# A hybrid trunk layer in fp32 on one core: the output projection's rows split in place in a ring of two slots, and the attention values of two head pairs copied together

## The chip, the cores and the metric

The kernel runs on one core of a Trainium2 chip. Its engines are TensorE (PE, matmuls; PEld is its weight load), VectorE (DVE), ScalarE (ACT), GpSimd (POOL) and SyncE (SP), which issues nearly all DMAs. Each engine, and each queue of issues, executes in the order in which the program was built. The metric is the time of one execution in microseconds (us).

## The reference: what is computed

One layer for 1024 tokens with 1024 channels, all float32:

```python
h = rmsnorm(x, ln1)
u_pool, gq, gk, gv, gg, ga, fq, fk, fv, ff = split(h @ w_in)
mix = concat(pool_mixer(u_pool), gla_mixer(gq, gk, gv, gg, ga), fox_mixer(fq, fk, fv, ff))
x = x + mix @ w_o
gate, up = split(rmsnorm(x, ln2) @ w_gu)
x = x + (silu(gate) * up) @ w_down
return rmsnorm(x, ln_f)
```

The pool mixer (256 channels) takes trailing means over 2, 4, 8 and 16 tokens, the gated linear attention (GLA, 4 heads of 64) runs over chunks of 64 tokens with a decayed state, and the forgetting attention ("fox", 8 heads of 64) is a causal softmax with an added decay `F_t - F_s`. The inner width of the FFN is 2816.

## The kernel before

**Products.** An fp32 matrix enters PE as a high half (rounded to float32r by ACT) and a low half (the raw value minus the high half, by DVE or POOL). A product is three matmuls: high by high, high by low, low by high. So each weight tile costs a load, one ACT rounding (line 118) and one subtraction (line 119) before PE can use it.

**Memory.** The large tiles are all of 128 partitions by 1024 floats. `G(name)` takes one of 33 slots from a list in the order in which slots were freed, and `free` gives it back. `R(name, tag)` takes the next slot of a ring: "p" has 6, "pp" 3, "fb" 2, "wr" (raw weights) 2, "w" (split weights) 4. A tile in a slot waits until the last use of the one before it is done. PSUM has banks "s" 3, "pt" 2, "o" 1 and "gm" 2; projections (`z...`, `psv`, `pxa`, `pxb`) all use the two "gm" banks.

**The program.** (1) Norm of x, its transposes `hT`, and the projection of the GLA values and the gates, up to about 60 us. (2) Pool inputs (`zp0`, `zp1`) and the GLA for head pairs A (j = 0) and B (j = 1): for each pair `keys` (`zgk`), `queries` (`zgq`) and `gates` (`zgg`). Small pieces of work are woven in between the matmuls of a projection: `state` (PE pkv, then a chain of 15 DVE updates of `St` at line 397), `within` (PE pat, then masked copies into `attb` at line 418), `outputs`, `turned`, and the pool's products (`py`, `pa`, `mh`). (3) `fox_values(0)`: the attention values of pairs 0 and 1, eight token blocks of 256 columns each (PE `psv0_0` to `psv0_7`), with pieces of GLA pair B between them. (4) For each pair p of fox heads: `fox_qk(p)` (`zq`, `zk`: projections whose results are split into q, k, kl) and `fox_attend(p)` (scores, softmax, transposes `pt`, the splits `pp` and the products `o`). PE fills the waits of a pair's attention with the projections of the next: psv1, zq2 and zk2 during pair 1, zq3 and zk3 during pair 2. (5) The output projection: `pxa` (first four blocks of `w_o`, with the tiles `mix`) and `pxb`. (6) Norm, FFN (`m`, 541 to 954 us), down projection (`d`, 954 to 1130 us), final norm.

**What the change touches.** `keep_wo(k)` (lines 279 to 284) splits the rows 128k to 128k+127 of `w_o`: load `wos{k}r`, round into `wos{k}h`, subtract into `wos{k}l`, and store both to a DRAM buffer `wod`, from which `fetch_wo` (line 289) takes them back for `pxa` and `pxb`. Each call takes three G slots, and gives them back when its reads are done. The eight calls follow `fox_values(0)` in the program. `fox_values` (lines 517 to 530) writes V tiles of one pair each, two per pair with four token blocks in a tile: for each token block and each pair one ACT copy (line 528, 128 x 128) and one DVE subtraction (line 529). The V tiles of a pair are freed when that pair's attention is done.

**What sets the order.** The kernel's text gives the program, and the tile framework's scheduler (`schedule_with_timeline_sim=True`) orders the instructions of all engines by its own estimate of when they become ready. Rows of engines can therefore move though the text that writes them did not.

## Time and profile before

| what | before |
|---|---|
| median of 3 runs | 1175.11 us (1174.69 to 1177.39) |
| profiled execution | 1175.42 us |
| its span in the trace | 1173.7 us |
| mean granted PE clock | 0.992 |
| PE busy | 1136.0 us (97%) |
| DVE busy | 828.2 us (71%) |
| ACT busy | 536.0 us (46%) |
| POOL busy | 340.4 us (29%) |
| HBM read, written | 105.09 MB, 44.34 MB |

The span is the part of the execution that the trace covers; the profiled time is 1.7 us longer. Busy shares overlap, since the engines work side by side. A row of waits names the instructions that stood, and the one whose end released them. In a row of the chain the time of an instruction is its own contribution to the end. A matmul row's "zq0p L152" is an instruction of line 152 that writes the tile zq0p.

### The profile page before, as it was taken

Reading aid. Unit: us, or ns where it says so; the run is one execution under the profiler, and the core shown is the slowest. Engines: PE = TensorE matmul, PEld = TensorE weight load, DVE = VectorE, ACT = ScalarE, POOL = GpSimd, SP = SyncE. Lnnn points to the kernel's source line nnn. Section 1 sums busy time; section 2 is a strip of 40 time slices with the busy share of each in tenths; the row PEclk is TensorE's granted clock in tenths of the full one; section 3 lists DMA queues with packets and bytes.
Section 4 is the critical chain, followed back from the end, with each engine's and each line's share of the span. In section 5 each row is a group of like instructions: output and inputs, shape, how many; then the busy total and the mean of one; then the engine's idle time right before and its main releaser. Section 6 shows DMA issues by size and latency. Waiting matters only on the chain.

```text
span 1173.7 us, 15953 instructions
## 1 busy us (share of the span) xinstructions
PE 1136.0 (97%) x5928; PEld 958.5 (82%) x5928; DVE 828.2 (71%) x1365; ACT 536.0 (46%) x970; POOL 340.4 (29%) x260
## 2 busy tenths in 40 slices
PE   6999998999999999998999999999999999999996
PEld 5877878889978888886888888888888888888875
DVE  6697364387746866579997767767686685876686
ACT  6454233466654644456453433444344344334345
POOL 2231123343322413210302221022201370660784
PEclk9999999999999999999999999999999999999999
DMA  7121184411203734431323332242314688333233
GB/s 250 37 73 52 59 295 174 176 39 35 91 18 126 305 132 159 173 112 46 117 86 129 101 115 88 101 134 82 135 54 152 224 322 293 103 95 102 86 112 143
DMA packets 57692, 150.45 MB, mean 128 GB/s; under 512 B 5080, under 2 KB 5512, under 8 KB 57616
## 3 DMA queue, kind: packets, MB, share of 16 engines
q1 hardware_dynamic: 57184, 147.87, 36.5%
q0 software_dynamic: 432, 1.57, 0.4%
q8 instruction: 46, 0.75, 0.3%
q14 instruction: 30, 0.25, 0.1%
HBM read 105.09 MB, written 44.34 MB: 127 GB/s over the span
## 4 chain that ended last, share of the span: by engine, by line
PE 76%; DVE 4%; DMA 1%; issue 1%; POOL 1%; ACT 1%; SPq 0%; POOLq 0%; DVEq 0%; ACTq 0%
PE m L774 36%; PE d L1030 15%; PE pxa L144 4%; PE pxb L144 3%; PE o L615 3%; PE pt L601 2%; PE psv L152 2%; PE s L575 1%; PE s L576 1%; PE zq3p L152 1%; PE zq0p L152 1%; PE zq2p L152 1%; PE zk1p L152 1%; PE zk2p L152 1%; PE zk0p L152 1%
## 5 line engine op out<-in xcount | busy, mean ns | idle before, releaser
L774 PE MATMUL m<-hA_0h,wr 128*128 128x512 f32 x616 | 214.7, 391 | 1.2 <-ACT hr L729 1.2
L774 PE MATMUL m<-hA_1h,wr 128*128 128x512 f32 x616 | 214.9, 389 | 0.0
L774 PEld LDWEIGHTS m<-hA_0h,wr 128*128 128x128 f32 x616 | 116.1, 189 | 25.8 <-ACT hr L729 1.6
L774 PEld LDWEIGHTS m<-hA_1h,wr 128*128 128x128 f32 x616 | 115.8, 188 | 24.2
L1030 PE MATMUL d<-lw,ha 128*128 128x512 f32 x308 | 119.9, 389 | 0.9 <-DVE lw L880 0.9
L774 PE MATMUL m<-hA_0l,wr 128*128 128x512 f32 x308 | 120.3, 391 | 0.0
L774 PE MATMUL m<-hA_1l,wr 128*128 128x512 f32 x308 | 119.9, 389 | 0.0
L1030 PE MATMUL d<-hw,ha 128*128 128x512 f32 x308 | 119.3, 389 | 0.0
L1030 PE MATMUL d<-hw,la 128*128 128x512 f32 x308 | 118.4, 389 | 0.0
L756 ACT ACTIVATE wr<-ws 128x512 fp32r<-128x512 f32 x110 | 69.5, 632 | 101.5 <-DVE ws L755 50.1
L826 POOL TENSOR_TENSOR cg<-cu,cu 128x512 f32<-128x512 f32 x11 | 19.7, 1795 | 302.8 <-DVE cu L803 266.7
L757 DVE TENSOR_TENSOR wr<-ws,wr 128x512 fp32r<-128x512 f32 x110 | 76.8, 704 | 20.6 <-ACT wr L756 20.5
L880 DVE TENSOR_TENSOR la<-ra,ha 128x1024 fp32r<-128x1024 f32 (+1 forms) x42 | 57.2, 1368 | 32.0 <-ACT ha L879 24.7
L590 POOL TENSOR_TENSOR pb<-pb,rl 128x128 f32<-128x128 f32 (+3 forms) x32 | 39.0, 1222 | 117.5 <-DVE rl L587 108.9
L872 POOL TENSOR_TENSOR rw<-wd,wd 128x512 f32<-128x512 f32 x33 | 59.0, 1815 | 47.7 <-PE d L1030 47.6
L879 ACT ACTIVATE ha<-ra 128x1024 fp32r<-128x1024 f32 (+1 forms) x42 | 41.3, 987 | 65.6 <-DMA ra<-cd 56.8
L1030 PEld LDWEIGHTS d<-lw,ha 128*128 128x128 f32 x308 | 57.8, 188 | 13.3 <-DVE lw L880 1.3
L604 DVE TENSOR_TENSOR pp<-pt,pp 128x512 fp32r<-128x512 f32 (+1 forms) x80 | 50.2, 631 | 25.7 <-ACT pp L603 25.3
L774 PEld LDWEIGHTS m<-hA_0l,wr 128*128 128x128 f32 x308 | 58.1, 189 | 12.0
L774 PEld LDWEIGHTS m<-hA_1l,wr 128*128 128x128 f32 x308 | 58.0, 188 | 12.0
L1030 PEld LDWEIGHTS d<-hw,la 128*128 128x128 f32 x308 | 57.8, 188 | 12.1
L1030 PEld LDWEIGHTS d<-hw,ha 128*128 128x128 f32 x308 | 57.8, 188 | 11.9
(398 smaller groups left out, 2690.6 us busy)
## 6 DMA issues: line engine op xcount, KB each, us to landing
ra<-cd SPq DMA_DIRECT2D x35, 512.0 KB, 3.9
wu<-in_w_gu_dram SPq DMA_DIRECT2D x22, 512.0 KB, 4.6
wg<-in_w_gu_dram SPq DMA_DIRECT2D x22, 512.0 KB, 3.7
wd<-in_w_down_dram SPq DMA_DIRECT2D x22, 512.0 KB, 6.4
mix<-mixs SPq DMA_DIRECT2D x14, 512.0 KB, 5.3
cd<-cg SPq DMA_DIRECT2D x11, 512.0 KB, 6.3
cd<-cs SPq DMA_DIRECT2D x11, 512.0 KB, 3.4
cd<-cu SPq DMA_DIRECT2D x11, 512.0 KB, 3.3
```

The costliest lines, as they stand in the source:

```text
L144: PE.matmul(ps, a, b, start=(n == 0), stop=(n == last))
L152: PE.matmul(ps, a, b, start=(i == 0 and n == 0), stop=(i == len(terms) - 1 and n == 2))
L590: POOL.tensor_tensor(out=pb[:, 0:W], in0=pb[:, 0:W], in1=rl[:, 0:1].broadcast_to([P, W]), op=ALU.mult)
L604: DVE.tensor_tensor(out=pp[:, 512:512 + w], in0=pt[:, 0:w], in1=f(pp[:, 0:w]), op=ALU.subtract)
L615: PE.matmul(*args, start=(kb == 0 and n_ == 0), stop=(last and n_ == 1))
L756: ACT.activation(hi, src, AF.Copy)
L757: DVE.tensor_tensor(out=lo, in0=src, in1=f(hi), op=ALU.subtract)
L774: PE.matmul(ps, a, b, start=(n == 0), stop=(n == 11))
L872: POOL.tensor_tensor(out=raw_[:, j * 512:j * 512 + 512], in0=wd[h0, j0 + j][:, e0, :], in1=wd[h1, j0 + j][:, e1, :], op=op)
L879: ACT.activation(hi[:, sl], src, AF.Copy)
L880: DVE.tensor_tensor(out=lo[:, sl], in0=src, in1=f(hi[:, sl]), op=ALU.subtract)
L1030: PE.matmul(banks[t], a[:, o], b[:, ns], start=(j0 + j == 0 and m == 0), stop=(j0 + j == NF // 2 - 1 and m == 2))
```

## The change

`keep_wo` takes two slots of the ring "fb" and no G slot: the raw rows land in the first, the high half goes into the second, and the low half is written over the raw rows. Both are stored. The ring has only these two slots, so the load of block k+1 can start when the low half of block k is stored. The same ring holds the squares of the first norm (before) and the decay sums that each attention pair broadcasts (`fb{p}_{a}`, behind). The eight calls stand earlier: two before the keys of B, two before its gates, four before `fox_values(0)`.

`fox_values` makes four V tiles that hold both pairs, with two token blocks in a tile, and copies both pairs of a token block at once (128 x 256): one ACT and one DVE instruction in place of two and two. The four tiles are freed together when the odd pair is done; before, a pair's two tiles were freed after that pair. While pair 2 and pair 3 are worked on, pair 2's values therefore stay two slots longer.

```diff
     def keep_wo(k):
 
-        hi, lo = load_g(w_o[k * P:(k + 1) * P, :], f"wos{k}", tag="G")
+        raw, hi = R(f"wos{k}", tag="fb"), R(f"wosh{k}", F32R, tag="fb")
+        SP.dma_start(raw, w_o[k * P:(k + 1) * P, :])
+        ACT.activation(hi, raw, AF.Copy)
+        DVE.tensor_tensor(out=raw, in0=raw, in1=f(hi), op=ALU.subtract)
         SP.dma_start(wod[k, :, 0], f(hi))
-        SP.dma_start(wod[k, :, 1], f(lo))
-        free(f"wos{k}h", f"wos{k}l")
+        SP.dma_start(wod[k, :, 1], raw)
...
-        V = [[G(f"v{2 * q + j}_{i}", F32R).rearrange("p (t h s e) -> p t h s e", t=4, h=2, s=2) for i in range(2)] for j in range(2)]
+        V = [G(f"v{q}_{i}", F32R).rearrange("p (t j h s e) -> p t j h s e", t=2, j=2, h=2, s=2) for i in range(4)]
...
-            for j in range(2):
-                v_ = V[j][tb // 4][:, tb % 4]
-                pv = ps[:, 128 * j:128 * j + 128].rearrange("p (h e) -> p h e", h=2)
-                ACT.activation(v_[:, :, 0], pv, AF.Copy)
-                DVE.tensor_tensor(out=v_[:, :, 1], in0=pv, in1=f(v_[:, :, 0]), op=ALU.subtract)
+            v_ = V[tb // 2][:, tb % 2]
+            pv = ps[:, 0:256].rearrange("p (j h e) -> p j h e", j=2, h=2)
+            ACT.activation(v_[:, :, :, 0], pv, AF.Copy)
+            DVE.tensor_tensor(out=v_[:, :, :, 1], in0=pv, in1=f(v_[:, :, :, 0]), op=ALU.subtract)
...
-                v_ = V[p % 2][kb // 4][:, kb % 4, a]
+                v_ = V[kb // 2][:, kb % 2, p % 2, a]
...
     B = Gla(1)
+    keep_wo(0)
+    keep_wo(1)
     B.keys((A.within(1) + A.outputs(0), A.outputs(1) + A.turned(0)))
     B.queries((A.turned(1) + pools[1], B.turn_keys()))
     free("misc")
+    keep_wo(2)
+    keep_wo(3)
     B.gates((B.state(), B.within(0)))
+    for k in range(4, 8):
+        keep_wo(k)
     o_ = [B.outputs(0), B.outputs(1)]
     V = fox_values(0, (B.within(1), o_[0][:1], o_[0][1:], o_[1][:1], o_[1][1:] + B.turned(0), B.turned(1), (), ()))
-    for k in range(8):
-        keep_wo(k)
...
-        done = [f"{n}{p}_{a}" for n in ("q", "k", "kl") for a in range(2)] + [f"v{p}_{i}" for i in range(2)]
+        done = [f"{n}{p}_{a}" for n in ("q", "k", "kl") for a in range(2)] + [f"v{p // 2}_{i}" for i in range(4) if p % 2]
         if p == 1:
             V = fox_values(1)
-            free(*[done.pop() for _ in range(2)])
+            free(*[done.pop() for _ in range(4)])
```

How the instructions stand now, at the three places of which the prediction speaks. In a row: the line, the operation, the output, the inputs, the shape; the number at a name's end is the tile's own.

ACT in the GLA of pair A, around the first half of its gates (`sg`) and the first pool product (`pa`, `mh`). Before:

```order
L368 ACTIVATE sg_997<-zgg0p_1005 128x512
L509 ACTIVATE pa_973<-py_0_1085,ch 128x512
L342 ACT_TABLE_LOAD
L342 ACTIVATE eq_1131<-d_1_1129 128x1024
L509 ACTIVATE pa_973<-py_1_1094,ch 128x512
L343 ACTIVATE d_1_1129<-d_1_1129 128x1024
L273 ACTIVATE mh_1097<-pa_973 128x1024
```

And in the change, where wos_1543 and wos_1550 are the sixth and the seventh block (k = 5 and 6):

```order
L283 ACTIVATE wosh_1544<-wos_1543 128x1024
L370 ACT_TABLE_LOAD
L370 ACTIVATE sg_997<-zgg0p_1005 128x512
L511 ACTIVATE pa_973<-py_0_1085,ch 128x512
L283 ACTIVATE wosh_1551<-wos_1550 128x1024
L344 ACT_TABLE_LOAD
L344 ACTIVATE eq_1131<-d_1_1129 128x1024
L511 ACTIVATE pa_973<-py_1_1094,ch 128x512
L345 ACTIVATE d_1_1129<-d_1_1129 128x1024
L273 ACTIVATE mh_1097<-pa_973 128x1024
```

The roundings of two blocks stand ahead of `sg`, `eq` and `mh`. On DVE the subtraction of the sixth block stands ahead of the first eight `St` updates, and that of the seventh ahead of the other seven.

DVE in `fox_values(0)`, from the second half of the copies into `attb` on. Before (wos6l is the low half of block k = 6):

```order
L418 COPY_PREDICATED attb_658<-gmask,pat_1_1_1538 128x512
L119 TENSOR_TENSOR wos6l<-wos6r,wos6h 128x1024
L529 TENSOR_TENSOR v_0_1508<-psv_0_1524,v_0_1508 128x2x64
L529 TENSOR_TENSOR v_0_1508<-psv_1_1565,v_0_1508 128x2x64
L529 TENSOR_TENSOR v_0_1510<-psv_0_1524,v_0_1510 128x2x64
L529 TENSOR_TENSOR v_0_1510<-psv_1_1565,v_0_1510 128x2x64
L452 TENSOR_REDUCE gss_1648<-on_0_1645 128x8
```

And in the change:

```order
L420 COPY_PREDICATED attb_658<-gmask,pat_1_1_1594 128x512
L530 TENSOR_TENSOR v_0_1564<-psv_0_1580,v_0_1564 128x4x64
L530 TENSOR_TENSOR v_0_1564<-psv_1_1619,v_0_1564 128x4x64
L530 TENSOR_TENSOR v_1_1565<-psv_2_1660,v_1_1565 128x4x64
L454 TENSOR_REDUCE gss_1700<-on_0_1697 128x8
```

No row of `wos` is left in this stage, on DVE, ACT or SP.

ACT at the end of pair 1, where the k rows empty the two banks of zk2 for zq3. Before (k_0 from the first bank stands further ahead of these rows):

```order
L543 ACTIVATE k_0_3408<-zk2p_3515 64x512
L618 ACTIVATE ot_1_2_3073<-o_1_2_3037 64x256
L603 ACTIVATE pp_1_3_0_3109<-pt_1_3_0_3108 128x512
L603 ACTIVATE pp_1_3_1_3121<-pt_1_3_1_3120 128x512
L603 ACTIVATE pp_1_3_2_3133<-pt_1_3_2_3132 128x512
L603 ACTIVATE pp_1_3_3_3145<-pt_1_3_3_3144 128x384
L618 ACTIVATE ot_1_3_3155<-o_1_3_3107 64x256
L543 ACTIVATE k_1_3409<-zk2p_3482 64x512
L543 ACTIVATE k_1_3409<-zk2p_3515 64x512
L273 ACTIVATE mh_3548<-y_2685 128x1024
```

And in the change:

```order
L604 ACTIVATE pp_1_3_3_3121<-pt_1_3_3_3120 128x384
L619 ACTIVATE ot_1_3_3131<-o_1_3_3083 64x256
L544 ACTIVATE k_0_3368<-zk2p_3442 64x512
L544 ACTIVATE k_0_3368<-zk2p_3475 64x512
L273 ACTIVATE mh_3508<-y_2661 128x1024
L544 ACTIVATE k_1_3369<-zk2p_3442 64x512
L544 ACTIVATE k_1_3369<-zk2p_3475 64x512
```

All four k rows stand behind the last `ot`; before, two did. On DVE the four kl rows stand in the same way behind the last `y`.

## The prediction

> **What bounds the kernel now.** I read the page first. TensorE (PE) is busy for nearly the whole span and owns most of the chain that ended last, so a change of this kind can pay only where PE stands still or runs at a lower granted clock, and can cost only by making PE stand still elsewhere.

> ```profile
> span 1173.7 us, 15953 instructions
> ...
> PE 1136.0 (97%) x5928; PEld 958.5 (82%) x5928; DVE 828.2 (71%) x1365; ACT 536.0 (46%) x970; POOL 340.4 (29%) x260
> ```

> Second, the waits of PE, one line per matmul group and what released it (total, times, longest):

> ```profile
> PE zq0p L152 <- DVE v L529: 3.5, 1, 3.5
> PE zq3p L152 <- DVE kl L544: 2.5, 1, 2.5
> PE pk L375 <- DVE d L351: 2.1, 1, 2.1
> PE psv L152 <- DVE v L529: 1.5, 1, 1.5
> PE pot L466 <- DVE on L456: 0.4, 1, 0.4
> ```

> Two of the five (zq0p, psv) wait for the copies of V, pot sits in the same stretch, zq3p is the end of attention pair 1 and pk is in the GLA stage. Third, stretches of the span: length, then busy time of PE, PEld, DVE, ACT, POOL, then PEclk, DMA share and GB/s.

> ```profile
> 60.00:100.00 40.00, 37.86 (x168) 30.28 (x167) 38.68 (x36) 16.16 (x21) 11.36 (x4) 1.00 0.20 67
> 110.00:120.00 10.00, 10.00 (x77) 7.43 (x74) 5.55 (x11) 7.64 (x8) 0.00 (x0) 1.00 0.27 107
> 170.00:180.00 10.00, 8.46 (x84) 8.15 (x83) 3.37 (x8) 2.42 (x7) 1.64 (x1) 0.83 0.56 224
> 200.00:210.00 10.00, 7.41 (x25) 5.94 (x26) 4.20 (x5) 2.34 (x5) 4.57 (x2) 0.83 0.91 331
> 260.00:300.00 40.00, 40.00 (x325) 39.30 (x324) 30.86 (x87) 25.71 (x60) 12.55 (x11) 1.00 0.09 28
> 350.00:360.00 10.00, 7.45 (x33) 6.10 (x31) 4.61 (x10) 2.62 (x4) 4.55 (x6) 0.83 0.32 122
> ```

> PE loses time in 170–180, 200–210 and 350–360, and there alone of these the granted clock is 0.83: a sixth of ten microseconds lost, as if the clock had been half for some 3.4 us. From 110 to 120 and from 260 to 300 PE is full. From 60 to 100 VectorE (DVE) is nearly full, 38.68 of 40. Fourth, the chain of waits (start, length, link) at the two ends:

> ```profile
> 198.68 1.05 ACT wos1h L118
> 199.75 2.58 DVE wos1l L119
> 202.59 12.81 PE zq0p L152 x48
> 215.40 11.05 PE zk0p L152 x48
> ...
> 349.67 0.99 PE o L615 x7
> 350.69 0.69 DVE kl L544
> 351.40 0.60 ACT k L543
> 352.45 0.70 DVE kl L544
> 353.19 6.19 PE zq3p L152 x19
> ```

> At 198 PE is kept from zq0p by a rounding and a subtraction of `wos1`, that is, by the work that the change moves. The same 48 matmuls take 12.81 us there and 11.05 right after: 1.76 us for the slow clock, beside the wait.

> **The change part by part.** *What it takes off the path.* With no `wos` work between the V copies, the psv and pot waits should go: 1.5 + 0.4 = 1.9 us. The slow clock of 170–180 follows that wait; a sixth of ten microseconds would be 1.7, and as PE was idle for part of it I take 1.4. The 3.5 of zq0p does not go whole, because its weight zq0 is split in the same moment, by a POOL subtraction that now becomes the last thing awaited:

> ```profile
> 198.91 2.35 POOL L119 TENSOR_TENSOR zq0l<-zq0r,zq0h 128x1024 fp32r<-128x1024 f32 x1 [7.11 <-issue]
> ```

> It ends at 201.26, 1.3 before zq0p starts at 202.59, and without DVE's 2.58-us subtraction beside it I expect it about 1 us shorter: 2.3 of the 3.5 gained, bounds 1.3 (POOL as slow as now) and 3.5. The slow clock after it goes with the longer wait; at 7 chances in 10, 1.2 of 1.76. Sum of gains: 1.9 + 1.4 + 2.3 + 1.2 = 6.8 us.

> *The merged copies* of V:

> ```profile
> L528 ACT ACTIVATE v<-psv x32: 255/277/280, 173.1 to 313.2; 128x128 fp32r<-128x128 f32 x32
> L529 DVE TENSOR_TENSOR v<-psv,v x32: 270/283/292, 174.4 to 313.9; 128x128 fp32r<-128x128 f32 x32
> L184 ACT ACTIVATE hT<-n1s x16: 367/384/386, 11.9 to 43.8; 128x256 fp32r<-128x256 f32 x16
> L185 DVE TENSOR_TENSOR hT<-n1s,hT x16: 349/414/426, 13.0 to 44.3; 128x256 fp32r<-128x256 f32 x16
> ```

> The rows are minimum/median/maximum in ns. Two ACT copies of 277 become one of about 384, two DVE subtractions of 283 one of about 414 (the nearest rows of that size, PSUM to SBUF): 16 x 0.17 = 2.7 us less on ACT, 16 x 0.15 = 2.4 us less on DVE. Half lies at 173–200, where it belongs to the gains above; the other half lies at 260–313, where PE is full, so it counts nothing.

> *What the eight splits of w_o cost at their new place.* In a ring of two slots the load of block k+1 waits until the low half of block k has landed in DRAM. Columns: queue, count, size, us to landing; then the subtraction.

> ```profile
> wos0r<-in_w_o_dram SPq DMA_DIRECT2D x1, 512.0 KB, 3.5
> wos1r<-in_w_o_dram SPq DMA_DIRECT2D x1, 512.0 KB, 4.7
> wod<-wos0l SPq DMA_DIRECT2D x1, 512.0 KB, 3.1
> wod<-wos6l SPq DMA_DIRECT2D x1, 512.0 KB, 2.6
> wod<-wos5l SPq DMA_DIRECT2D x1, 512.0 KB, 4.7
> L119 DVE TENSOR_TENSOR wos0l<-wos0r,wos0h x1: 1226/1226/1226, 156.1 to 156.1; 128x1024 fp32r<-128x1024 f32 x1
> ```

> One link, from the end of one rounding to the end of the next: subtraction 1.23 + store 3.1 + load 3.5 + rounding 1.05, with some 0.3 for hand-overs (my estimate), 9.2 us. The two early DMA rows, wos0r and wos0l, are the nearest, since 110–120 has a DMA share of 0.27 and 200–210 one of 0.91. A link of the shortest rows (2.6 and 3.5) takes 8.7, of the longest (4.7 and 4.7) 12.0. Four rows of DVE's timeline that matter for the walk:

> ```profile
> 94.36 1.22 DVE L351 TENSOR_TENSOR d<-gk,d 128x1024 f32<-128x1024 f32 x1
> 107.13 2.55 DVE L397 SCALAR_TENSOR_TENSOR St<-St,dec,pkv 128x64 f32<-128x64 f32 x8
> 110.58 2.18 DVE L397 SCALAR_TENSOR_TENSOR St<-St,dec,pkv 128x64 f32<-128x64 f32 x7 [0.90 <-PE pkv L393]
> 121.72 1.34 DVE L418 COPY_PREDICATED attb<-gmask,pat 128x512 f32<-128x512 int8 x2 [2.65 <-PE pat L415]
> ```

> I walked the new order on DVE and ACT with these lengths. The first two blocks fall into the norm stage, the third and fourth (76.5 and 86.5 on ACT and DVE by my walk) before pk; there other pool work is ordered behind `d`, so pk's 2.1 stays about as it is. The fifth rounding ends near 95.7, and each later one is a link on: the sixth near 108.1 after DVE's subtraction of the fifth at 99–100.2, the seventh near 117.4, the eighth near 126.7. The sixth's subtraction stands ahead of the first eight St updates: they end at about 111.9 instead of 109.7. The seventh's stands ahead of the last seven: 120.9 instead of 112.8. Behind the seventh rounding ACT has the table load, eq, pa and mh of the pool; DVE's pa<-pa,mh waits for mh, and the second attb copy behind it ends near 124.1. PE needs the banks: the second pkv group +1.6, the second pat group +1.85, and pk +0.25: +3.7 us in a stretch that is full today. Bounds: about +1 with the shortest links; +9.7 with the longest, where the two or three links in play are 2.8 longer each and some is absorbed. A wait of 1.6 to 1.9 can also bring the slow clock, as the 1.5 of psv did: I add 0.6 (about four chances in ten of 1.4).

> [...]

> *The queue of SP and the ring's other users.* All 24 DMA issues of the blocks move ahead in SP's queue, which runs in order: a `wos` load that waits for a store holds back the weight loads behind it.

> ```profile
> L118 ACT ACTIVATE zgg1h<-zgg1r x1: 1057/1057/1057, 132.0 to 132.0; 128x1024 fp32r<-128x1024 f32 x1
> ```

> The nearest is zgg1r, behind the load of the sixth block: by the walk it leaves at about 104 and lands, at 4.7, near 109, while its rounding comes at 132.0. The rows of the decay sums that the same ring broadcasts for pair 0 come behind the eighth block, near 131, and pair 0's scores only follow zq0 and zk0, which fill PE until 226 (215.40 + 11.05). I count nothing for both; that cover would be gone if the ring ended some 20 us later than I walk it.

> [...]

> *Pair 1's end.* With fewer copies around psv1 the fillers are used up sooner, and two of the K copies now stand behind the last ot copy on ACT. Today PE waits from the last `o` (350.66) to 353.19, 2.5 us, for kl, k and kl in turn. In the new order four DVE kl rows and the k rows come after it: 0.60 + 0.70 + 0.70 more, partly overlapped, about 4.3 instead of 2.5; with the smaller filler, +2.4. Bounds 0 (another wait hides it) and +3. The slow clock of 350–360 is there already.

> *Smaller terms.*

> ```profile
> mix<-mixs SPq DMA_DIRECT2D x8, 512.0 KB, 10.3
> 467.00 7.58 DMA wo6h<-wod
> ```

> The first mix slice is asked for when zk3 runs and takes 10.3; PE reaches pxa a little sooner behind it, +0.9 (0 to 2). V of pairs 2 and 3 stays until pair 3 is done, two slots fewer, so the last w_o halves are fetched later, and the chain already waits for wo6h at 467: +0.5 (0 to 1).

> *Sum.* 3.7 + 0.6 + 2.4 + 0.9 + 0.5 = 8.1 lost, 6.8 gained: +1.3. The profiled execution took 1175.42 us (1173.7 of span and 1.7 around it), 0.3 above the median of 1175.11; so 1176.7 by its own time, 1176.4 against the median.

> **The rivals.** *Faster: the ring hides.* If stores and loads land fast and the kl tail is no longer, the losses are 1.0 + 0.5: 1175.1 − 6.8 + 1.5 = 1169.8. For it: ACT is used 16.16 of 40 us at 60–100 and the DMA queues are a fifth busy. Against it: DVE is full there. *Slower: the chain of the ring becomes the bound at 100–125.* DVE and ACT execute in order, so a rounding that waits for its load holds eq, mh and St behind it, and through them pat and pkv. From links of about 11 us on it decides: 9.7 + 1.5 + 2.4 + 0.9 + 0.5 − 6.8 = +8.2, 1183.3. For it: wos1r and wos5l with 4.7 each; against it: they stand where the DMA share is 0.9. *The change does not do what it says:* zq0p waits as long for zq0l, at the slow clock (3.5 of the gain is lost): 1179.9.

> **How the numbers follow.** This kernel's measurement can tell 0.3%, 3.5 us, from no change: faster is under 1171.6, slower over 1178.6. Likeliest, gains and losses cancel: 0.47, at 1176.4, own range 1172.5 to 1180. Ring hidden: 0.28, around 1169.8. Ring the bound: 0.19, around 1183. No gain at zq0p: 0.06. Faster takes all but a little of the second and 0.03 of the first: 0.29. Slower takes the third, most of the fourth and 0.07 of the first: 0.30. Same is the rest, 0.41. The range reaches to the rivals: 1169 to 1182.5.

> **What would show it.** Right: the psv and zq0p waits for v are gone, zq0p waits about 1.2 for POOL zq0l, PEclk is 1.00 in 170–180 and near it in 200–210; ACT stands idle before the fifth to seventh `wosh` with a DMA as releaser, new PE waits of 1.6 to 1.9 stand near 110 and 122, and zq3p waits near 4.3 for kl. Wrong: no PE idle at 100–125 (then the first rival), or more than 6 us of it (then the second); a zq0p wait unchanged; or a difference in the FFN, where I expect none.

## The result, and the profile after

| what | before | change |
|---|---|---|
| median of 4 runs each | 1175.95 us (1174.69 to 1177.39) | 1183.68 us (1181.89 to 1185.19) |
| change against before | 1 | 1.0067, 95% interval 1.0047 to 1.0086 |
| profiled execution, its span | 1175.42 us, 1173.7 us | 1183.37 us, 1181.3 us |

The change costs 7.7 us. The likeliest outcome of the forecast was 1176.4, no difference to tell; the result lies 1.2 above the upper end of the range.

Where the time went, step by step. Each row below is the start or the end of one group of PE's matmuls in a trace, minus the same in the trace of before, in us. "Same again" is the change's order of instructions, built and profiled a second time (experiment 2); "ring alone" has the ring and the old V copies (experiment 1).

| point on PE | change | same again | ring alone |
|---|---|---|---|
| end of zgk0 (GLA keys of A) | -2.5 | -0.5 | -1.4 |
| end of zgg1 (gates of B) | +6.2 | +2.4 | +1.4 |
| start of zq0 | -1.2 | -5.0 | -5.8 |
| end of zk1 | -1.5 | -5.3 | -6.1 |
| end of zq3 (after pair 1's end) | +0.2 | -3.1 | -6.0 |
| end of pxb (output projection) | +7.7 | +6.0 | -6.2 |
| end of d (down projection) | +7.0 | +5.9 | -6.7 |

What a stage costs is the difference of two rows. The shift at zgk0 is older than the change's work there: over the 17 traces of this document it runs from -2.5 to +0.1, and in the change's trace 1.7 of the 2.5 stand already at PE's first matmul (8.65 us, 10.37 before). So the change loses 8.7 us (2.9 the second time) in the early stage, from zgk0 to zgg1, gains 7.4 between zgg1 and zq0 both times, loses 1.7 to 2.2 at pair 1's end and 7.5 to 9.1 in the output projection. From there to the end of `d`, FFN and down projection, the shift moves by less than 1 us.

First the waits of PE in the change (total, times, longest), to be laid beside those of before in the prediction:

```profile
PE pxb L144 <- DMA mix<-mixs: 2.5, 1, 2.5
PE pat L417 <- DVE attb L420: 2.1, 2, 1.6
PE pxa L144 <- DMA mix<-mixs: 2.0, 2, 1.5
PE pk L377 <- DVE d L353: 1.8, 1, 1.8
PE s L576 <- POOL k L547: 1.8, 1, 1.8
PE zq3p L152 <- DVE kl L545: 1.8, 1, 1.8
PE pt L602 <- DVE pp L605: 1.6, 3, 0.7
...
PE pxb L144 <- DMA wo4l<-wod: 0.8, 1, 0.8
PE pxb L144 <- DMA wo5h<-wod: 0.8, 1, 0.8
PE pkv L395 <- DVE St L399: 0.7, 1, 0.7
PE zq0p L152 <- POOL zq0l L119: 0.6, 1, 0.6
PE zq0p L152 <- DVE v L530: 0.4, 1, 0.4
```

The psv and pot waits are gone and zq0p's 3.5 has become 0.6 + 0.4: the gain is there. New are attb and St early, the `k` of POOL at pair 1's end, the transposes `pt` behind a split `pp` (0.7 at 345 us, the other two while the output projection runs), and four lines whose releaser is a DMA, all of the output projection.

Stretches of the change (busy time of PE, PEld, DVE, ACT, POOL, then PEclk, DMA share, GB/s):

```profile
100.00:120.00 20.00, 18.82 (x112) 13.77 (x112) 12.33 (x22) 10.71 (x12) 3.97 (x2) 1.00 0.51 185
120.00:130.00 10.00, 8.42 (x60) 7.43 (x60) 5.21 (x6) 4.54 (x7) 0.00 (x0) 0.59 0.81 267
170.00:180.00 10.00, 10.00 (x99) 9.61 (x98) 2.92 (x6) 0.77 (x2) 1.69 (x1) 1.00 0.19 54
200.00:210.00 10.00, 9.01 (x45) 7.10 (x44) 1.89 (x3) 3.07 (x5) 4.73 (x2) 1.00 0.60 210
340.00:360.00 20.00, 15.27 (x82) 12.16 (x80) 9.07 (x14) 8.32 (x15) 7.94 (x9) 0.83 0.21 79
430.00:470.00 40.00, 38.14 (x223) 32.78 (x222) 27.04 (x63) 19.55 (x40) 10.21 (x9) 1.00 0.46 159
470.00:500.00 30.00, 25.30 (x145) 21.30 (x144) 12.90 (x21) 9.77 (x21) 4.35 (x8) 1.00 0.64 228
```

And three of the same stretches before:

```profile
340.00:360.00 20.00, 16.76 (x89) 13.80 (x88) 7.92 (x15) 6.72 (x11) 7.53 (x8) 0.91 0.16 61
430.00:470.00 40.00, 40.00 (x234) 34.96 (x232) 27.55 (x62) 19.19 (x38) 11.34 (x9) 1.00 0.61 206
470.00:500.00 30.00, 29.78 (x171) 25.44 (x170) 16.29 (x25) 13.61 (x31) 5.95 (x10) 1.00 0.45 165
```

At 170 to 180 PE is now full (10.00 of 10 us) at a granted clock of 1.00. At 430 to 500, where the forecast saw next to nothing, PE lost 6.3 us of busy time against before (1.86 and 4.48). The chain of waits of the change (start, length, link) says what it stood for:

```profile
437.71 1.07 ACT mh L273
438.80 2.69 DMA mixs<-mh
441.50 4.68 DMA mix<-mixs
446.23 1.65 PE pxa L144 x6
...
470.79 7.47 DMA wo5h<-wod
478.40 0.70 PE pxb L144 x2
...
483.37 4.21 DMA mix<-mixs
487.72 11.15 PE pxb L144 x48
```

Four transfers stand on the path: a store with the load behind it, a half of `w_o`, and one more slice of `mix`. In the second profile the granted clock was 0.94 at 470 to 500 as well, half for 3.41 us from 484.28 on, which is most of the step from 7.5 to 9.1. Why the loads are late is seen on SP, which issues them. The issues of the last halves of `w_o` before (start, length; `wo4l` is the low half of block 4):

```profile
429.94 0.33 SPq L289 DMA_DIRECT2D wo4h<-wod  x1
430.62 0.33 SPq L289 DMA_DIRECT2D wo4l<-wod  x1
434.48 0.32 SPq L289 DMA_DIRECT2D wo5h<-wod  x1
466.08 0.33 SPq L289 DMA_DIRECT2D wo5l<-wod  x1
```

And in the change:

```profile
431.43 0.33 SPq L291 DMA_DIRECT2D wo4h<-wod  x1
...
470.24 0.42 SPq L291 DMA_DIRECT2D wo4l<-wod  x1
470.79 0.35 SPq L291 DMA_DIRECT2D wo5h<-wod  x1
...
472.85 0.32 SPq L291 DMA_DIRECT2D wo5l<-wod  x1
474.34 0.32 SPq L291 DMA_DIRECT2D wo6h<-wod  x1
...
483.37 0.52 SPq L648 DMA_DIRECT2D mix<-mixs  x1
```

`wo4l` and `wo5h` are asked for 39.6 and 36.3 us later than before, in one batch from 469.86 to 474.34 that asks for seven halves. The mix slice of `pxb`'s third block (`mix6_0`) is asked for only at 483.37, when pair 3's last product `o` has ended (483.35).

### The profile page after: what moved, and what is told of

It is laid out like the page before. It is cut to its first block, busy times and chain, and to the rows that moved or that the text cites. A ratio compares the mean times of both kernels' runs of the same rounds, so it can differ in the third digit from the quotient of the medians.

```text
span 1181.3 us, 15908 instructions
## 1 busy us (share of the span) xinstructions
PE 1138.5 (96%) x5928; PEld 960.6 (81%) x5928; DVE 824.0 (70%) x1349; ACT 531.5 (45%) x954; POOL 336.3 (28%) x260
## 3 DMA queue, kind: packets, MB, share of 16 engines
q0 software_dynamic: 432, 1.57, 0.4%
## 4 chain that ended last, share of the span: by engine, by line
PE 62%; DMA 3%; DVE 3%; ACT 1%; issue 1%; POOL 1%; POOLq 0%; DVEq 0%; ACTq 0%
PE m L779 35%; PE d L1035 15%; PE pxa L144 3%; PE pxb L144 3%; DMA mix<-mixs 2%; PE zq3p L152 1%; PE pt L602 1%; PE o L616 1%; PE zk3p L152 1%; DMA wo5h<-wod 1%; PE n2pt L732 1%; PE s L577 1%; PE s L576 0%; DVE lw L885 0%; POOL f_r L107 0%
## 5 line engine op out<-in xcount | busy, mean ns | idle before, releaser
L585 ACT ACTIVATE pb<-pb,mn 128x128 f32<-128x128 f32 (+3 forms) x64 | 49.4, 773 | 42.4 <-DVE mn L581 41.9
L1035 PEld LDWEIGHTS d<-hw,ha 128*128 128x128 f32 x308 | 57.8, 188 | 11.9
## 6 DMA issues: line engine op xcount, KB each, us to landing
ra<-cd SPq DMA_DIRECT2D x35, 512.0 KB, 3.9
wu<-in_w_gu_dram SPq DMA_DIRECT2D x22, 512.0 KB, 4.6
wg<-in_w_gu_dram SPq DMA_DIRECT2D x22, 512.0 KB, 3.7
wd<-in_w_down_dram SPq DMA_DIRECT2D x22, 512.0 KB, 6.9
mix<-mixs SPq DMA_DIRECT2D x14, 512.0 KB, 6.6
cd<-cg SPq DMA_DIRECT2D x11, 512.0 KB, 6.4
cd<-cs SPq DMA_DIRECT2D x11, 512.0 KB, 3.4
cd<-cu SPq DMA_DIRECT2D x11, 512.0 KB, 3.4
```

What stands on the lines that cost most here:

```text
L585: ACT.activation(pb[:, 0:W], pb[:, 0:W], AF.Exp, bias=mn[:, 0:1], scale=-1.0, accum_out=l[:, i:i + 1])
L1035: PE.matmul(banks[t], a[:, o], b[:, ns], start=(j0 + j == 0 and m == 0), stop=(j0 + j == NF // 2 - 1 and m == 2))
```

## The experiments

Letters in the quoted expectations name the theories as they stood before that run. A: two losses, the ring's wait with the slow clock near 120 us and the missing slots in the output projection. B: the ring near 120 us is all of the loss. C: the V tiles' slots, held longer, are the loss at pair 1's end and in the output projection. D: the blocks come early because the ring needs no G slot, and the attb wait near 120 us comes and goes from one execution to the next. Ratios are to the kernel before, with 95% intervals.

### 1. Each half of the change alone

The V part alone (the four tiles for two pairs, the merged copies, `free` after the odd pair; `keep_wo` as before):

> The kernel before with the V part of the change alone (shared tiles, merged copies, four freed at once); w_o is split as before. Theory A (two losses: the ring's wait and slow clock near 120 us, and the two slots missing in the output projection; one gain at zq0): no loss near 120, the wo4l/wo5h loads still come only at 470 us and PE waits 4 to 6 us for wo and mix tiles in pxb, a gain of 1 to 3 at the V copies: +3 to +7 us against the kernel before, about 1180. Theory B (all of the loss is the ring near 120 us): same as before or up to 3 us faster, 1173 to 1176.

Measured: 1185.61 us (1183.81 to 1187.45), ratio 1.0086 (1.0064 to 1.0107).

The ring alone, run twice under two names (the whole `keep_wo` part of the diff and the moved calls; V as before):

> The ring of two slots alone, at the changed places; V as before. Theory A: PE waits for attb near 120 us and the clock is halved there for about 10 us, +9; the gain of about 7 at psv and zq0 is there; the output projection is as before: -1 to +3 us against the kernel before, 1175 to 1179. Theory B: the V part is innocent, so this is as slow as the whole change, 1183.

> The ring alone once more, for its spread. Theory D (whether PE waits for attb near 120 us, and then runs at half clock for about 10 us, differs between executions by the landing of one load and by the phase of the clock): most runs 1168 to 1171, some 1173 to 1176. Rival (the wait does not occur without the V part): all within 1168 to 1171.

Measured: 1169.78 (1168.59 to 1170.78), ratio 0.9950 (0.9935 to 0.9966), and 1171.08 (1170.37 to 1171.66), 0.9952 (0.9940 to 0.9964).

The ring gains 5 to 6 us and the V part loses 9 to 10. The ring is not the cause of the loss; theory A had -1 to +3 for it and B the whole loss, and neither had the V part alone as slow as the whole change. In the trace of the V part alone the shift is -0.5 at zgg1, -2.5 at zq0, +1.9 at zq3, +10.7 at the end of pxb: the loss stands at pair 1's end (2.6) and in the output projection (8.8), with 1.7 more between zq0 and the end of zk1. With the ring alone both are nil. The gain between zgg1 and zq0 is 7.2 us with the old copies and 7.4 with the merged ones: once the `wos` work has left this stage, the merged copies bring nothing measurable (beside that work, in the V part alone, zq0 gains 2.0 on zgg1).

### 2. The calls of `keep_wo` back at their old place

```diff
-    keep_wo(0)
-    keep_wo(1)
...
     V = fox_values(0, ...)
+    for k in range(8):
+        keep_wo(k)
```

> The whole change with the eight calls of keep_wo put back behind fox_values(0), where they stood before. The scheduler builds the same rows in the same order on every engine as for the change, so theory D (the ring's freedom from G slots, not the calls' place, brings the blocks forward) expects the time of the change: 1179 to 1185, and about 8 us less in the runs where PE does not wait for attb. Rival (the place matters): 1170 to 1176.

Measured: 1182.44 (1181.60 to 1187.46), ratio 1.0064 (1.0044 to 1.0084). The order of instructions on all five engines came out as in the change, row for row. The moved lines of the diff have no effect: it is the ring that lets the scheduler pull the blocks forward, by theory D because it needs no G slot. The run therefore is a second profile of the same order, and the early stage differs by 5.8 us between the two (8.7 and 2.9). How is taken up in the last two sections.

### 3. The early stage relieved

PE's `within` pieces of A, which feed attb, moved to the second half of zgk1, in the change and in the ring alone:

```diff
-    B.keys((A.within(1) + A.outputs(0), A.outputs(1) + A.turned(0)))
+    B.keys(((), 3 * [lambda: None] + A.within(1) + A.outputs(0) + A.outputs(1) + A.turned(0)))
```

> The whole change with one piece of PE's order moved: the second pat products and the first outputs of GLA pair A stand in the second half of zgk1 instead of the first, so PE has other matmuls while DVE is late with attb; the ring and the orders of ACT and DVE around it are as in the change. Theory A (the wait for attb brings the slow clock, about 5 us of it): no attb wait over 0.5 us, granted clock 1.00 from 120 to 132, 5 to 8 us less than the whole change, 1176 to 1179. Rival (the small matmuls of pat and po bring the slow clock by themselves, or the wait turns up elsewhere): clock still below 0.9 in some stretch between 115 and 135, at most 2 us less, 1182.

> The ring alone with the second pat products and the first outputs of GLA pair A moved to the second half of zgk1: the candidate for a kernel faster than both. Theory C (the wait for attb comes and goes with the landing of one load, and in the ring alone did not come): no different from the ring alone within 2 us, 1168 to 1171. Rival (the ring still loses some 3 us near 120 us): 1166 to 1168.

Measured: 1181.33 (1180.44 to 1185.55), ratio 1.0055 (1.0037 to 1.0073); and with the ring alone 1171.07 (1169.45 to 1176.55), 0.9963 (0.9944 to 0.9983). In the trace of the first, zgg1 ends 1.7 late, where the change's profile had 6.2 and its second one 2.4, and the granted clock is 1.00 at 120 to 130 (0.59 in the change); a new wait of zgk1p for ACT's `sg` takes 1.6 of it. From zgk0 on, its early stage loses some 3 us, as in the second profile of the change. From zq3 to the end of pxb the loss stays 8.0. Even with the attb wait gone the change stays slower than before, so that wait is not what makes it slow; theory A had expected 1176 to 1179. To the ring alone the edit gives nothing.

### 4. The V slots held longer, without the merged tiles

All three start from the ring alone, with two tiles per pair and single copies, and only the `free` moves: pair 2's tiles freed after pair 3; pair 0's freed after pair 1; both. For both:

```diff
-        done = ... + [f"v{p}_{i}" for i in range(2)]
+        done = ... + [f"v{k}_{i}" for k in {0: (), 1: (0, 1), 2: (), 3: (2, 3)}[p] for i in range(2)]
...
-            free(*[done.pop() for _ in range(2)])
+            free(*[done.pop() for _ in range(4)])
```

> The ring alone with one thing of the V part added: the two tiles of pair 2's values are given back only after pair 3, as in the change; copies and tiles are as before the change. Theory C (two missing slots delay the loads of the last w_o blocks past 460 us, and PE waits for them in pxb): waits of 3 to 6 us for wo and mix tiles in pxa and pxb, 6 to 8 us more than the ring alone (1169.8): 1176 to 1178. Rival (the cost in the output projection comes from the merged copies or the moved fillers): under 2 us more, 1170 to 1171.5.

> The ring alone with pair 0's value tiles given back only after pair 1, as in the change, so that all four tiles k2 and kl2 fall on slots of values that pair 1's last product still reads. Theory C: PE waits for POOL k and DVE kl before pair 2 (about 4 us in all instead of 2.5), two windows of halved clock instead of one near 350: 2 to 3 us more than the ring alone, 1171.5 to 1173. Rival (fillers used up sooner by cheaper copies, as the prediction had it): no more than 0.5 us more, 1169.5 to 1170.3.

> The ring alone with both holds: the slots of the change without its merged copies. Theory C: the sum of the two, 8 to 11 us more than the ring alone, 1178 to 1181; what is left to the whole change (1183.7) is the wait and the halved clock near 120 us, at most 5. Rival (merging itself costs): under 1175.

| tiles held | median (range) | ratio (interval) | loss at pair 1's end | loss from zq3 to end of pxb |
|---|---|---|---|---|
| none (ring alone) | 1169.78 (1168.59 to 1170.78) | 0.9950 (0.9935 to 0.9966) | 0.0 | -0.2 |
| pair 0's | 1173.88 (1171.83 to 1178.18) | 0.9988 (0.9973 to 1.0003) | 2.5 | 0.5 |
| pair 2's | 1175.36 (1173.00 to 1179.43) | 0.9999 (0.9982 to 1.0015) | 1.2 | 2.7 |
| both | 1177.83 (1176.28 to 1185.10) | 1.0024 (1.0005 to 1.0043) | 1.8 | 6.0 |
| both, merged tiles (the change) | 1183.68 (1181.89 to 1185.19) | 1.0067 (1.0047 to 1.0086) | 1.7 | 7.5 |

The last two columns are differences of shifts in one trace each, as in the table of the result; the medians hold the spread of the early stage too. Holding alone makes about 6 of the 7.5 to 9.1 us of the output projection, with no merged copy in the kernel. It is not additive: 0.5 and 2.7 apart, 6.0 together. By the order of `G` and `free`, holding pair 2's tiles alone already gives `wo4l`, `wo5h`, `wo5l` and `mix3_1` the predecessors that they have in the change, and `wo4l` is asked for at 467.54 there; yet PE waits 1.6 for it and for no mix slice, where with both held it waits 1.9 in pxa as well. Why pair 0's tiles add so much to that is not settled.

Pair 0's tiles bring the loss at pair 1's end by themselves. PE's waits there with pair 0's tiles held:

```profile
PE zq3p L152 <- DVE kl L546: 2.2, 1, 2.2
...
PE s L577 <- POOL k L548: 1.8, 1, 1.8
```

And with the ring alone:

```profile
PE zq3p L152 <- DVE kl L546: 2.5, 1, 2.5
```

The `s` wait is the new one, the same as in the change. By the order of `G` and `free`, the four tiles of k2 and kl2 all take slots of V's first four when these are freed at pair 1's end; before, only kl2's two did. That all eight copies out of zk2's banks then wait for pair 1's last product follows from this order.

The fourth of this group is the change itself, with pairs 2 and 3 back in tiles of their own that are freed one pair at a time (pairs 0 and 1 keep the shared tiles and the merged copies):

> The whole change, but with the values of pairs 2 and 3 in tiles of their own pair, copied one by one as before (pairs 0 and 1 stay merged), so that the two slots come free after pair 2. Theory A: the waits for wo and mix in pxb go from about 5 us to under 1, 5 to 8 us less than the whole change: 1176 to 1179. Theory B: no more than 2 us from the whole change, 1182 to 1184.

Measured: 1174.23 (1171.77 to 1181.03), ratio 0.9989 (0.9972 to 1.0007), under the 1176 to 1179 of theory A. The loss from zq3 to the end of pxb is 0.9 in its trace, 1.8 at pair 1's end. The shared tiles of pairs 2 and 3 are the part that makes the change slower than before.

### 5. Which slots, and how many

One exchange in the change's list of slots: `mix6_0` goes to an idle slot of ring "w" and not to the one of `v1_0`, the first shared tile of pairs 2 and 3, which is read until pair 3 is done:

```diff
+    late, spare = where["v1_0"], rings["w"][0]
...
+    i_, j_ = idle.index(late), idle.index(spare)
+    idle[i_], idle[j_] = spare, late
```

> The whole change with one slot exchanged: mix6 of the first half no longer falls on a slot of values that pair 3 reads to its end, but on an idle ring slot. Theory C: the wait of 2.5 us for that mix tile in pxb goes, 2 to 3 us less than the change: 1179 to 1180.5. Rival (another load ends the wait at the same time): 1182.

Measured: 1178.00 (1177.07 to 1182.84), ratio 1.0028 (1.0016 to 1.0041), some 4 us less than the change. PE no longer waits for a mix tile in pxb, and is busy for 28.09 of 30 us at 470 to 500 (25.30 in the change); the loss at 430 to 470 stays (37.72, and 38.14 in the change):

```profile
430.00:470.00 40.00, 37.72 (x219) 32.22 (x218) 26.01 (x60) 18.99 (x40) 10.86 (x10) 1.00 0.47 160
470.00:500.00 30.00, 28.09 (x156) 23.51 (x154) 14.49 (x23) 11.52 (x25) 4.46 (x9) 1.00 0.56 209
```

This one place is what the merged tiles add over the held ones. With both pairs' tiles held but not merged, `mix6_0` lies by the order of `free` on a tile of pair 2 alone, whose last reader is pair 2; the merged tile in the same place in the list holds pair 3's values too, and is read until pair 3 is done.

If the number of slots were all, more of them would heal it. The six slots of the rings "wr" and "w" were given to the common list before the second half of the mix tiles, in the change, in the ring alone, and with six blocks in the ring:

```diff
+        if g:
+            idle[:0] = rings.pop("wr") + rings.pop("w")
...
-    for tag in ("wr", "w", "p", "pp", "fb"):
+    for tag in ("p", "pp", "fb"):
```

> The whole change, with the six ring slots for weights (wr and w, idle after zk3) handed to the general list before the second half of the mix tiles instead of before pxb. Theory C (scarcity of slots): no wait for wo or mix tiles over 1 us in pxa and pxb, 6 to 9 us less than the change (1182): 1173 to 1176. Rival (moved fillers, order): at most 2 us less, 1180 to 1182.

> The ring alone with the same six slots handed out early. Theory C: no slot was missing there, so no more than 1.5 us from the ring alone (1170 to 1171): 1169 to 1171. Rival (the slots bring a gain of their own): 1165 to 1168.

> The ring for blocks 0 to 5 (6 and 7 in G slots at the old place) with the six slots handed out early: the candidate for the fastest. Theory C: as that kernel without the slots, 1168 to 1170. Rival: 1164 to 1167.

Measured: 1180.51 (1177.67 to 1186.27), ratio 1.0046 (1.0028 to 1.0064); 1174.65 (1170.51 to 1180.73), 0.9993 (0.9975 to 1.0012); 1173.41 (1169.14 to 1174.73), 0.9970 (0.9959 to 0.9981). More slots helped the change by 2 to 3 us in the medians, with intervals that overlap, where theory C had expected 6 to 9; and they made the ring alone some 4 us slower and the ring of six blocks (1169.98 without them, experiment 6) some 3. In the ring alone with these slots, the row of PE at the start of pxb (start, length, and in brackets the idle time before it and its releaser):

```profile
471.16 0.50 PE L144 MATMUL pxb<-wo4h,mix 128*128 128x512 f32 x1 [2.77 <-DMA mix<-mixs]
```

By the order of `G` and `free`, `mix4_0`, `mix5_0` and `mix6_0` get slots of the first half's weights in this run (`wo2h`, `wo2l`, `wo3h`), which pxa reads until 463.3 to 464.4; in the ring alone they got those of `k3_0`, `k3_1` and `kl3_0`, which the scores read until 458.5 at the latest. The load that pxb's first product waits for is asked for at 463.92 and lands at 471.12. So more slots move the succession too, and what decides is which earlier reader a tile's slot had. Only for `mix6_0` was this tried by an exchange of one slot; for `wo4l`, `wo5h` and `mix3_1` it is read from the order of slots and from the times of the loads.

### 6. A shorter ring

The ring for the first six blocks, or the first five, the rest through G slots as before; V as before:

> The ring alone for blocks 0 to 5; blocks 6 and 7 take G slots and stand behind fox_values(0), as before the change, so that no rounding of w_o stands ahead of eq and mh on ACT, and no subtraction between the St updates. Theory D: no attb wait in any run, nothing lost from 104 to 135; the late blocks cost at most 2 us at zq0: 1166 to 1170. Rival (blocks 6 and 7 among the V copies bring the old waits back): 1171 to 1175.

> As the one before, with blocks 0 to 4 in the ring and 5 to 7 in G slots. Theory D: nothing lost from 98 to 135, but three blocks among the V copies: 1166 to 1171. Rival: 1172 to 1176, most of the old waits at psv and zq0 are back.

Measured: 1169.98 (1168.37 to 1170.53), ratio 0.9941 (0.9928 to 0.9953); and 1170.70 (1167.92 to 1172.11), 0.9945 (0.9930 to 0.9960). Both are faster than the kernel before and than the change, by 0.6%, and cannot be told from the ring alone.

## Why the prediction was wrong, point by point

**What bounds the kernel, and the gains: right.** 6.8 us were expected from psv, pot, zq0p and the two slow stretches; 7.4 were measured twice, and the waits went as described, zq0p keeping 0.6 for zq0l where 1.2 was expected. No run shows the 1 us that the text took off zq0l's subtraction for standing without DVE's beside it: it took 2.38 us in the change, 2.35 before. The half of the merged copies' saving that the text put at 173 to 200 is not needed for it: with the old copies the gain is 7.2.

**The early stage: right in mechanism, and between the two cases in size.** The forecast was +3.7 and 0.6 for the clock, 4.3; the two profiles of the same order had 2.9 and 8.7. The link was 10.5 us (from the rounding that ends at 104.37 to the one that ends at 114.90) where 9.2 was worked out, and mh stood behind the seventh rounding as in the walk. In the change's trace, ACT first, then DVE (in brackets the idle time and the releaser):

```profile
90.90 1.06 ACT L283 ACTIVATE wosh<-wos 128x1024 fp32r<-128x1024 f32 x1 [6.66 <-DMA wos<-in_w_o_dram]
103.31 1.06 ACT L283 ACTIVATE wosh<-wos 128x1024 fp32r<-128x1024 f32 x1 [1.67 <-DMA wos<-in_w_o_dram]
113.84 1.06 ACT L283 ACTIVATE wosh<-wos 128x1024 fp32r<-128x1024 f32 x1 [6.98 <-DMA wos<-in_w_o_dram]
118.70 1.04 ACT L273 ACTIVATE mh<-pa 128x1024 fp32r<-128x1024 f32 x1
```

```profile
114.93 1.23 DVE L284 TENSOR_TENSOR wos<-wos,wosh 128x1024 f32<-128x1024 f32 x1 [6.26 <-ACT wosh L283]
116.08 2.17 DVE L399 SCALAR_TENSOR_TENSOR St<-St,dec,pkv 128x64 f32<-128x64 f32 x7
120.92 0.72 DVE L420 COPY_PREDICATED attb<-gmask,pat 128x512 f32<-128x512 int8 x1
```

The second attb copy ended at 121.64, before the 124.1 of the walk, and the waits on PE were 0.7 (pkv) and 2.1 (pat) where 1.6 and 1.85 were worked out. The price of the clock was too small. Eleven traces have the change's order of PE up to the end of zgg1 (the change's two, its three variants of experiments 4 and 5, the ring alone twice and with more slots, and the three with tiles held): from zgk0 on, seven of them lose 2.6 to 3.0 us and four lose 6.9 to 8.7, and only in these four does half clock begin at 121 to 126, for 6.8 us in two of them and 10.2 in the other two. So four chances in ten was about right, and 1.4 us was not: the four lose 4 to 6 us more than the seven.

**Pair 1's end: right in size, by luck in part.** +2.4 was forecast, 1.7 to 2.2 measured. The text read rightly that the k and kl copies stand behind the last product, but gave the rest to fillers used up sooner by fewer copies; pair 0's held tiles alone bring 2.5 with the old copies, so the slots put the copies there. There is no zq3p of 4.3 either: `s` waited 1.8 for `k` and zq3p 1.8 for `kl`. And the half clock there lasts 6.83 us (from 350.45), where it lasted 3.41 before (from 353.73), which the text had counted as unchanged.

**The output projection: the step that failed.** "two slots fewer, so the last w_o halves are fetched later ... +0.5 (0 to 1)" and "+0.9 (0 to 2)" for the first mix slice: 1.4 together, 7.5 to 9.1 measured. The mix slice did cost 0.5 (a wait of pxa at 395.41); the term of the two slots is the one that was mis-sized. Forecast at 0.5, it came to some 7 to 9. The step took the two slots for a short delay of the last halves, on top of a wait that was there. But slots are given out from a list in order of release: two slots less move every later tile to another predecessor. By the order of `G` and `free`, `wo4l`, `wo5h` and `wo5l`, which before lay on the slots of mix2_0, mix3_0 and mix0_1, now lie on those of mix0_1, mix1_1 and mix2_1, which pxa reads to its end; mix3_1 waits for the store of mh6, which begins at 438.8, and mix6_0 for `v1_0`, read to the end of pair 3. Adding the measured 6.1 to 7.7 above the 1.4 to the predicted 1176.4 gives 1182.5 to 1184.1, and the two medians of this order are 1182.44 and 1183.68. The fit is closer than it should be: the other differences from the forecast, the shift up to zgk0 among them, add up to -0.5 in the change's profile and to -3.1 in the second. Without this term's excess both would have come out below the forecast, by up to 3 us, so it is the error.

**The rivals.** "The ring becomes the bound" named the right time (1183.3) for the wrong reason: the ring alone is faster than before. "The ring hides" named the time of the ring alone (1169.8 against 1169.78 and 1171.08), though not of the change, and by luck in part: the ring alone still loses 2.8 early. "The change does not do what it says" did not occur, as zq0p shows. A rival in which the succession of slots delays pxb was missing. The sign that the text set, "a difference in the FFN", did not appear beyond 1 us.

## What to carry to other kernels

Where tiles take slots in order of release, holding two of them longer is no local matter: write down, for each load behind them, whose slot it gets before and after, and when that one's last reader ends, since the load cannot start sooner. Ask of each half of a change what it does alone; here a gain of 0.5% was buried under a loss of 0.9% in one diff. One order built twice differed by 5.8 us in one stage, with 10.24 us of half clock there in one execution and none in the other, so one profile is not enough to price a stage.

## What the runs showed of the hardware

```profile
118.35:121.75 3.40, 1.31 (x10) 1.03 (x9) 2.52 (x4) 3.38 (x4) 0.00 (x0) 1.00 0.23 48
121.76:125.16 3.40, 3.40 (x15) 3.18 (x16) 0.98 (x1) 1.74 (x3) 0.00 (x0) 0.50 0.93 347
125.17:128.57 3.40, 3.40 (x28) 2.97 (x28) 2.47 (x3) 0.73 (x2) 0.00 (x0) 0.50 0.85 280
128.59:131.99 3.40, 3.40 (x24) 2.68 (x25) 0.86 (x2) 0.66 (x2) 0.65 (x1) 0.50 1.00 357
132.00:135.40 3.40, 3.40 (x24) 2.83 (x23) 0.76 (x2) 0.00 (x0) 0.99 (x1) 1.00 0.57 216
```

The same order, built again:

```profile
119.05:122.46 3.41, 2.47 (x15) 1.77 (x14) 2.54 (x4) 3.39 (x4) 0.00 (x0) 1.00 0.40 53
122.46:125.88 3.42, 3.42 (x38) 3.07 (x39) 1.02 (x1) 1.86 (x4) 0.00 (x0) 1.00 0.89 339
```

In the first, PE was busy for 1.31 of 3.40 us in one stretch, and the next three ran at half; in the second, PE came 2 us later to the same copies, waited less, the stretch held 2.47, and the clock stayed at 1.00. Cut in this way, the traces of before and the change have 280 stretches at full clock from 60 to 560 us. The seven that were followed by half clock held 0.47 to 1.87 us of busy PE. The other 273 held 1.57 or more, and only two of them less than 1.87: 1.57 from 91.04 and 1.62 from 483.57, both in the change. The half clock from 121.75 lasted 10.24 us although PE was busy throughout (3.40 of 3.40 us in each of the three stretches), and some 10.2 in the trace with both pairs' tiles held (0.61 at 120 to 130, 0.88 at 130 to 140). In the change some 7 of these 10.24 us were the small products of the GLA (`po` and `pat`, 64 wide or 64 deep), and whether their size is why was not tested.

The length of a wait did not price it: the psv wait of 1.5 us before was followed by half clock (from 176.24), the pk wait of 1.8 in the change was not, and the same pk wait in the ring alone, 1.9, was (from 95.79; 0.96 at 60 to 100). There PE comes later for it to the copies into attb, and no wait for them follows.

**Not settled.** The second profile of the order had 1.6 us of lost busy time at 100 to 130 and no half clock, but 2.9 us of shift there; the remaining 1.3 have no row.
